# A decoder block on one core: tokens placed 32 bytes below the weights' phase, V's weight rows padded to 320, the root's table loaded ahead, and two steps of the first MLP chunk moved

## The chip, the cores and the metric

The kernel runs on one core of one Trainium2 chip. Its time is the device time of one execution in microseconds; a run's figure is the median of several executions. Nearly all matrix products take float32r operands, each split into a high and a low part, and add three products of these parts.

## The reference

One layer of a hybrid decoder on 512 tokens of width 1024, all in float32. What is computed, cut to what matters here:

```python
h = rms_norm(x, norm_mix)
proj = h @ w_in                       # split into u, q, six k/v pieces, g_nsa, g_merge
y_pool = pool_mixer(u, w_pool, pool_scale)
y_nsa = nsa_mixer(q, kc, vc, ks, vs, kw, vw, g_nsa, ...)   # compressed, selected, window branch
g_a, g_b = split(sigmoid(g_merge))
merged = g_a * (y_pool @ w_proj_pool) + g_b * (y_nsa @ w_proj_nsa)
x = x + merged @ w_out
h = rms_norm(x, norm_mlp)
x = x + square(relu(h @ w_ff1)) @ w_ff2          # 1024 -> 4096 -> 1024
return rms_norm(x, norm_final)
```

## The kernel before

The work runs in three stages on one TensorE instruction stream. **Stage 1** (to about 167 us) normalizes x, turns it into columns (R1 holds the high parts, R2 the low parts of all 8 row blocks of 512 tokens) and multiplies it by the columns of `w_in`. **Stage 2** (to about 378 us) is the attention, with the products for the merge gates filled in between. **Stage 3** forms the merged activations, multiplies them by `w_out` (the layer "o"), normalizes (lines 1416 to 1437) and runs the MLP in four chunks `c` of 1024 hidden columns.

Each product is written as TensorE's three terms (high by high, high by low, low by high; `split_products`, line 403). The output projection and both MLP products use a Strassen-Winograd scheme: an operand's four quarters 11, 12, 21, 22 and their sums T1 to T4 meet the weights' quarters A11, A12, A21, A22 and the sums S1 to S4, in seven products instead of eight. In an MLP chunk the first product (`Group`, line 1507; `product`, line 1494) runs for two groups `g` of 512 hidden columns each: the weights are the stationary operand, the tokens the moving one in pieces of 256 columns, 24 matmuls per product, all issued by line 1526. The second one (`Wide`, line 1265; line 1290) has the hidden activations stationary and the weights moving, 512 columns at a time.

**Weights.** `WL` (line 91) lists the weights in the order of use, `LD` the loads. `emit_load` (line 220) starts a DMA on SP's queue into a tile of 1024 elements per partition, of a ring of `RAW` = 4 tiles and a fifth in stage 3 (line 1240); a tile comes free by `give_back`. `emit_prep_half` (line 328) splits a landed weight: ACT copies the high part (line 358, or 312 for the MLP's), DVE or POOL subtracts for the low part (360, 314). `ahead` (line 375) does this up to three weights before their use. Some S sums are made ahead in DRAM by DMAs with addition (line 275); others are made in place, by adding a held raw tile to the next (line 324): A12 and S2 of a group are added to give S4. In the first chunk the order of use is A11, A12, S1, S3, S2 for both groups, then A22 and S4 of one group after the other (line 134).

**Where the operands lie.** The constants' pool holds, in this order, `ident`, two small tiles, R1, R2, `MA` and `GB` (16,384 bytes per partition each), `identR`; then come the raw ring and the weights' high and low tiles. R1 and R2 each have `STEP` = 32 elements more than their 8 x 512. Stage 1 reads R1 from its start and R2 from 128 bytes on; stage 3 (`Rf`, line 1237) reads R1 from 128 bytes on and R2 from its start. T2, T3 and T4 have tiles of their own (line 1486), the first with the same 32 elements ahead of it. V's weights are three tiles with rows of 304 elements (line 111; the products are `project_v`, line 830).

**The end of the output projection.** `by_tile` (line 1300) does the last products of the projection tile by tile; after each, `to_fm` (line 1416) takes the square sums, the root (`normed`, line 1249: `Sqrt` on ACT, `reciprocal` on DVE, two multiplications on DVE by line 1255), eight transposes on TensorE (1426) and the splits of their results. `sums_x` (line 1439) then forms T1, T3, T2 and T4 of the tokens: a difference or sum on DVE (1443), the high part on ACT (1444), the low part on DVE (1446).

**The group's rest.** `Group.main` (line 1538) waits for S1, S2 and S3, then forms u2 (line 1546) and u3 (1547) on DVE; A22 adds onto the bank that u3 reads, so it waits for u3 (`NEEDS`, line 1534) and for T4.

**What sets the order.** The generators in `side` are stepped between matmuls (`step_side`, line 417), which gives the order in which instructions are written. The framework's planner then puts each engine's instructions in order by this priority and by its own costs and due times; `tc.issue_after(x)` pins what is written inside it behind `x` on `x`'s engine. A function needing another table on ACT gets a load of that table in front of it.

Of the kernel before, what the change touches and what calls it, by code (L numbers as in the profile page):

```python
# [13 lines left out]
F32 = mybir.dt.float32  # L14
# [13 lines left out]
LAG, PLAG = 5, 2  # L28
P_BUFS, PT_BUFS = 6, 3
CMP_AT = 4  # L30
STEP = 32
BIG = 1e30
EPS = 1e-6

# [29 lines left out]
def trunk(ctx: ExitStack, tc: tile.TileContext, A, out):  # L64
# [17 lines left out]
    ident = cp.tile([128, 128], F32, name="ident")  # L82
    eps_t = cp.tile([128, 1], F32, name="eps_t")
    tick = cp.tile([128, 1], F32, name="tick")
    RR = [cp.tile([128, 8 * S + STEP], FR, name=n) for n in ("R1", "R2")]
    R1, R2 = (R[:, i * STEP:i * STEP + 8 * S].rearrange("p (j t) -> p j t", j=8) for i, R in enumerate(RR))
    MA = cp.tile([128, 8, S], F32, name="MA")
    GB = cp.tile([128, 8, S], F32, name="GB")
    GBf = GB.rearrange("p j t -> p (j t)")
# [104 lines left out]
    for c in range(4):  # L194
# [16 lines left out]
            turn.append((g, o))  # L211
        add_turn(2, c, of, turn)
    dest = {}

    raws, hls = {}, {}
    st = {"load": 0, "prep": 0, "use": 0, "kept": 0, "pairs": 0, "sums": 0, "hold": 0}
    spare, slots_hl = [], []
    held, begun = {}, deque()

    def emit_load():  # L220

        i = st["load"]
        if i >= len(LD):
            return False
        segs = LD[i]
        a = segs[0][0].shape[1]
        b = sum(s.shape[2] for s, _ in segs)
        assert a * b <= 1024
        if not by_name() or st["kept"] < RAW:
            st["kept"] += by_name()  # L230
            t = wp.tile([128, 1024], F32, tag="raw", bufs=RAW, name=f"raw{i}")
        elif spare:
            t = spare.pop(0)
        else:
            return False
        st["load"] += 1
        v = t[:, :a * b].rearrange("p (a b) -> p a b", a=a)
        for s, o in segs:
            began = nc.sync.dma_start(v[:, :, o:o + s.shape[2]], s)
        raws[i] = (t, a, b)  # L240
        for _ in range(sums_after(i)):
            make_sum(began)
        if i >= len(P1) + len(FILL2) + 4 and (len(begun) > 2 or begun and st["sums"] == len(jobs)):
            add_sum()
        return True
# [49 lines left out]
    def group_steps(i):  # L295

        key, at = WL[i]
        if i in PLUS:
            while st["load"] <= PLUS[i]:
                assert emit_load()  # L300
            t = raws.pop(PLUS[i])[0]
            DVE.tensor_tensor(t, t, held[key], op=ALU.add)
            give_back(held.pop(key))
            yield
        elif isinstance(at, str):
            t = held.pop(key)
        else:
            while st["load"] <= at:
                assert emit_load()
            t = raws.pop(at)[0]  # L310
        h, l = slot_of(i)
        ACT.activation(h, t, AF.Copy)  # L312
        yield
        DVE.tensor_tensor(l, t, h.bitcast(F32), op=ALU.subtract)  # L314
        a = 2 if key[-3] == "2" else 4
        hls[i] = tuple(x.rearrange("p (a b) -> p a b", a=a) for x in (h, l))
        to = SUM_OF.get(key)
        if to is None:
            give_back(t)
        elif to not in held:  # L320
            held[to] = t
        else:
            yield
            DVE.tensor_tensor(t, t, held[to], op=ALU.add)
            give_back(held[to])
            held[to] = t

    def emit_prep_half():

        i = st["prep"]  # L330
        if i >= len(WL):
            return
        if WL[i][0][0] in "AS":
            if "gen" not in part:
                part["gen"] = group_steps(i)
            if next(part["gen"], True):
                part.clear()
                st["prep"] += 1
            return
        at = WL[i][1]  # L340
        if "h" not in part:
            while st["load"] <= at:
                assert emit_load()
            if WL[i][0] in dest:
                h, l = dest[WL[i][0]][:2]
            else:
                h, l = slot_of(i)
            part.update(h=h, l=l, half=0)
        h, l = part["h"], part["l"]
        t, a, b = raws[at]  # L350
        n = a * b
        cut = (a // 2) * b
        sl = slice(0, cut) if part["half"] == 0 else slice(cut, n)
        if sl.stop > sl.start:
            if mode["first"] is POOL:
                POOL.tensor_scalar(h[:, sl], t[:, sl], 1.0, 1.0, op0=ALU.mult, op1=ALU.mult)
            else:
                ACT.activation(h[:, sl], t[:, sl], AF.Copy)  # L358
            eng = POOL if mode["first"] or part["half"] and mode["pool"] else DVE
            eng.tensor_tensor(l[:, sl], t[:, sl], h[:, sl].bitcast(F32), op=ALU.subtract)  # L360
        if part["half"] == 0:
            part["half"] = 1
            return
        part.clear()
        st["prep"] += 1
        raws.pop(at)
        if st["load"] > RAW + MLP0:
            give_back(t)
        else:
            emit_load()  # L370
            if st["kept"] == RAW:
                give_back()
        hls[i] = (h[:, :n].rearrange("p (a b) -> p a b", a=a), l[:, :n].rearrange("p (a b) -> p a b", a=a))

    def ahead():

# [857 lines left out]
    XQ = {b: quarter(MAf, i) for i, b in enumerate(("11", "12", "21", "22"))}  # L1234
    XT = quarter(GBf, 0)
    have = set()
    Rf = [R[:, STEP - i * STEP:STEP - i * STEP + 8 * S] for i, R in enumerate(RR)]
    XB = {b: [quarter(f, i) for f in Rf] for i, b in enumerate(("11", "21", "22", "T1"))}
    slots_hl.insert(0, [p4.tile([128, 1024], FR, name=f"w3{e}") for e in "hl"])
    give_back(p4.tile([128, 1024], F32, name="raw5"))  # L1240
# [111 lines left out]
    with ExitStack() as c3:  # L1352
# [13 lines left out]
            return x.rearrange("p (h t) -> p h t", h=2)  # L1366

        def split(x, hi, lo):
            ACT.activation(hi, x, AF.Copy, scale=0.5)
            DVE.scalar_tensor_tensor(lo, x, 0.5, hi.bitcast(F32), op0=ALU.mult, op1=ALU.subtract)  # L1370

        def split_m(j):
            x, n = GB[:, j, :], j % 4
# [4 lines left out]
            y = GB[:, n, 256:]  # L1378
            DVE.tensor_tensor(y, x[:, 256:], y, op=ALU.subtract)
            split(two(x), *(m[:, :, n, :] for m in M2))  # L1380
            split(y, *(m[:, n, :] for m in MB["T3"]))

        def split_t(j):
            x, n = GB[:, j, :], j % 4
# [14 lines left out]
        for j in range(2, 8):  # L1399
            def post(ps, j=j):  # L1400
                merge(j, ps)
                for n in (0, 1) if j == 2 else (j - 1,):
                    split_m(n)
                if j > 2:
                    split_t(j - 3)
                if j == 7:
                    split_m(7)
            fm3(f"pn{j}", post, OT)
        formed.update(("11", "21", "22", "T1", "T3"))
        side.append(rest())  # L1410
# [28 lines left out]
        def sums_x():  # L1439

            for o, d, x, y in (("T1", XT, XQ["11"], XQ["12"]), ("T3", XQ["12"], XQ["22"], XQ["12"]),
                               ("T2", XQ["11"], XQ["22"], XT), ("T4", XQ["21"], XQ["11"], XQ["21"])):
                DVE.tensor_tensor(d, x, y, op=ALU.add if o == "T2" else ALU.subtract)
                ACT.activation(XB[o][0], d, AF.Copy)
                yield
# [40 lines left out]
    for b in ("T2", "T3", "T4"):  # L1486
        XB[b] = []
        for e in "HL":
            n = STEP if b + e == "T2H" else 0
            t = a4.tile([128, 1024 + n], FR, name=f"x{b}{e}")  # L1490
            XB[b].append(t[:, n:].rearrange("p (k t) -> p k t", k=4))
    YF = {"11": quarter(GBf, 0), "12": quarter(GBf, 1), "21": quarter(GBf, 2), "22": quarter(MAf, 1)}
# [14 lines left out]
    class Group:  # L1507
# [30 lines left out]
        def main(self):  # L1538
# [4 lines left out]
            while not {"S1", "S2", "S3"} <= self.done:  # L1543
                yield
            yield
            DVE.tensor_tensor(self.u2, self.s, self.ps["b"], op=ALU.subtract)
            DVE.tensor_tensor(self.u3, self.ps["c"], self.u2, op=ALU.add)
            self.done.add("u3")
            yield
            DVE.tensor_tensor(self.u3, self.ps["d"], self.u3, op=ALU.add)  # L1550
# [186 lines left out]
```

## Time and profile before

| | |
|---|---|
| median of 3 runs | 787.26 us (786.75 to 787.62) |
| the profiled execution | 787.36 us |
| its span, from the first to the last instruction | 785.5 us |
| TensorE matmul, busy | 765.9 us (98%), 4517 matmuls |
| VectorE, busy | 639.4 us (81%) |
| ScalarE, busy | 498.9 us (64%) |
| GpSimd, busy | 186.4 us (24%) |
| mean granted TensorE clock | 0.996 |

A row of the timeline gives the start in us from the span's start, the duration in us, the engine, the line, the operation, the output and the inputs with the shapes, and in brackets the idle time before it with what ended it. Rows of one kind that follow each other are merged (x2 and so on). Matmuls are pipelined and their ends are modelled, so their durations overlap; the pace is the distance of two starts. A row of the table by windows gives the window, its length, each engine's busy time and instructions, the granted clock of TensorE, the DMA engines' share and GB/s.

### The profile page before, as it was taken

Reading aid. Unit: us, or ns where it says so; the run is one execution under the profiler, and the core shown is the slowest. Engines: PE = TensorE matmul, PEld = TensorE weight load, DVE = VectorE, ACT = ScalarE, POOL = GpSimd, SP = SyncE. Lnnn points to the kernel's source line nnn. Section 1 sums busy time; section 2 is a strip of 40 time slices with the busy share of each in tenths; the row PEclk is TensorE's granted clock in tenths of the full one; section 3 lists DMA queues with packets and bytes.
Section 4 is the critical chain, followed back from the end, with each engine's and each line's share of the span. In section 5 each row is a group of like instructions: output and inputs, shape, how many; then the busy total and the mean of one; then the engine's idle time right before and its main releaser. Section 6 shows DMA issues by size and latency. Waiting matters only on the chain. (4 is left out here: it accounts for less than half of the span.)

```text
span 785.5 us, 12873 instructions
## 1 busy us (share of the span) xinstructions
PE 765.9 (98%) x4517; PEld 671.2 (85%) x4517; DVE 639.4 (81%) x1207; ACT 498.9 (64%) x970; POOL 186.4 (24%) x253
## 2 busy tenths in 40 slices
PE   8999999999999999999999899999999999999995
PEld 6889888888888888988887799979998999799974
DVE  6788666436999888897698999997899789978897
ACT  6756543335998888897346685944783478346755
POOL 4000000026766776673110100111111101000002
PEclk9999999999999999999999999999999999999999
DMA  9454743487655866434997978989897989785552
GB/s 306 136 158 121 185 125 104 125 216 213 135 118 126 166 151 135 114 82 78 360 264 221 285 188 234 300 227 295 257 290 226 292 255 280 182 268 163 165 184 108
DMA packets 120156, 153.88 MB, mean 196 GB/s; under 512 B 5878, under 2 KB 88474, under 8 KB 119835
## 3 DMA queue, kind: packets, MB, share of 16 engines
q1 hardware_dynamic: 99514, 125.06, 48.6%
q0 software_dynamic: 20288, 27.27, 22.5%
q8 instruction: 36, 0.59, 0.3%
q10 hardware_dynamic: 288, 0.72, 0.3%
q14 instruction: 30, 0.24, 0.1%
HBM read 148.31 MB, written 56.62 MB: 261 GB/s over the span
## 5 line engine op out<-in xcount | busy, mean ns | idle before, releaser
L401 PE MATMUL psF<-R,wh 128*128 128x512 f32 x512 | 162.2, 398 | 0.0
L312 ACT ACTIVATE wh<-raw 128x1024 fp32r<-128x1024 f32 x84 | 88.5, 1056 | 80.6 <-PE psB L1526 28.2
L314 DVE TENSOR_TENSOR wl<-raw,wh 128x1024 fp32r<-128x1024 f32 x84 | 103.7, 1239 | 23.8 <-ACT wh L312 23.8
L279 POOL DMA_DIRECT2D S<-w_ff x44 | 48.6, 1104 | 292.0 <-DMA S<-w_ff 191.6
L401 PEld LDWEIGHTS psF<-R,wh 128*128 128x128 f32 x512 | 92.1, 188 | 16.3
L401 PE MATMUL psF<-R,wl 128*128 128x512 f32 x256 | 100.2, 392 | 0.0
L1085 POOL TENSOR_SCALAR P<-P,sm,GT 128x128 f32<-128x128 f32 (+3 forms) x128 | 82.6, 666 | 53.6 <-DVE sm L1075 37.6
L358 ACT ACTIVATE wh<-raw 128x512 fp32r<-128x512 f32 (+1 forms) x90 | 54.5, 620 | 62.1 <-PE psF L401 44.0
L1069 ACT ACTIVATE P<-P,sm 128x128 f32<-128x128 f32 (+3 forms) x128 | 71.1, 558 | 10.1 <-DVE sm L1059 9.4
L312 ACT ACTIVATE w3h<-raw 128x1024 fp32r<-128x1024 f32 x42 | 44.4, 1058 | 43.8 <-PE psB L1526 14.3
L360 DVE TENSOR_TENSOR wl<-raw,wh 128x512 fp32r<-128x512 f32 (+1 forms) x75 | 52.2, 700 | 20.7 <-ACT wh L358 20.6
L1059 DVE CUSTOM_DVE_ANT_0 P<-psS,cst 128x128 f32<-128x128 f32 (+3 forms) x128 | 59.7, 483 | 8.1 <-PE psT L1102 6.1
L1526 PE MATMUL psB<-R,wh 128*128 128x256 f32 x352 | 64.5, 283 | 0.0
L1117 DVE TENSOR_TENSOR PT<-psT,PT 128x512 fp32r<-128x512 f32 (+2 forms) x96 | 56.6, 596 | 3.8 <-ACT PT L1113 3.0
L314 DVE TENSOR_TENSOR w3l<-raw,w3h 128x1024 fp32r<-128x1024 f32 x42 | 51.2, 1218 | 8.4 <-ACT w3h L312 8.4
L401 PEld LDWEIGHTS psF<-R,wl 128*128 128x128 f32 x256 | 48.0, 188 | 10.4
L1113 ACT ACTIVATE PT<-psT 128x512 fp32r<-128x512 f32 (+2 forms) x96 | 49.4, 519 | 8.8 <-PE psT L1102 7.8
L1526 PEld LDWEIGHTS psB<-R,wh 128*128 128x128 f32 x352 | 54.7, 189 | 0.2
L1102 PE MATMUL psT<-ident,P 128*128 128x128 f32 x320 | 50.9, 273 | 1.1 <-DVE PT L1117 1.1
L1526 PE MATMUL psB<-R,wl 128*128 128x256 f32 x176 | 50.0, 284 | 0.0
L1102 PEld LDWEIGHTS psT<-ident,P 128*128 128x128 f32 x320 | 39.5, 140 | 10.0 <-issue 1.8
L1136 PE MATMUL psO<-PT,VV 128*128 128x256 f32 x320 | 47.7, 286 | 0.0
(451 smaller groups left out, 2010.0 us busy)
## 6 DMA issues: line engine op xcount, KB each, us to landing
raw<-w_ff SPq DMA_DIRECT2D x54, 512.0 KB, 6.0
S<-w_ff POOLq DMA_DIRECT2D x44, 512.0 KB, 8.3
raw<-S SPq DMA_DIRECT2D x44, 512.0 KB, 5.7
raw<-w_in SPq DMA_DIRECT2D x32, 512.0 KB, 4.1
S<-w_ff SPq DMA_DIRECT2D x32, 512.0 KB, 7.4
S<-S SPq DMA_DIRECT2D x12, 512.0 KB, 5.8
S_2o<-w_out POOLq DMA_DIRECT2D x8, 512.0 KB, 6.6
raw<-w_proj_nsa SPq DMA_DIRECT2D x8, 512.0 KB, 5.2
```

The costliest lines, as they stand in the source:

```text
L312: ACT.activation(h, t, AF.Copy)
L314: DVE.tensor_tensor(l, t, h.bitcast(F32), op=ALU.subtract)
L358: ACT.activation(h[:, sl], t[:, sl], AF.Copy)
L360: eng.tensor_tensor(l[:, sl], t[:, sl], h[:, sl].bitcast(F32), op=ALU.subtract)
L401: PE.matmul(ps, a, b, start=first and j == 0, stop=last and j == n - 1, skip_group_check=True)
L1059: DVE.tensor_tensor_reduce(out=P[:, o:o + n].rearrange("p (a c) -> p a c", c=128), in0=s, in1=m, scale=1.0, scalar=3e38, op0=ALU.add, op1= ...
L1069: last_exp[:] = [ACT.activation(c, c, AF.Exp, bias=sm[:, 0, e:e + 1], scale=-1.0, accum_out=sm[:, 1, e:e + 1])]
L1085: r = POOL.tensor_scalar(P[:, o:o + n], P[:, o:o + n], sm[:, 2, e:e + 1], GT[:, qb, c + e:c + e + 1], op0=ALU.mult, op1=ALU.mult)
L1102: PE.transpose(pt[:, 128 * j:128 * j + 128], P[:, 128 * j:128 * j + 128], ident)
L1113: ACT.activation(dH, src, AF.Copy)
L1117: DVE.tensor_tensor(dL, src, dH.bitcast(F32), op=ALU.subtract)
L1526: PE.matmul(out, w[u][:, k, 128 * f:128 * f + 128], XB[x][v][:, k, :], **kw)
```

## The change

It has five parts.

- **Addresses.** `STEP` is 8 elements (32 bytes). R1 gets 64 elements more than 8 x 512, R2 gets 8. Stage 1 reads both from 32 bytes on, stage 3 reads both from their starts. T2's own tile has 56 elements ahead of it, so that all seven token operands keep one phase.
- **V's rows.** A weight's rows are laid out at a stride rounded up to 64 elements: V's 304 become 320. The halves of a split are now whole rows. For all other weights the stride is what it was.
- **The root's table.** Behind the ACT part of the last `split_m` of the projection (the split of T3, for j = 7) a `Sqrt` of one column is written, which brings the table load with it.
- **A12's first weight** (A12 of chunk 0, group 0) is loaded into `GBf[:, 1024:2048]`, rows 2 and 3 of the gates' buffer, and no longer into a tile of the ring; its load is pinned behind the load before it. After S2 has been added to it, that place is not given to the ring.
- **T4 later.** T4's three steps are written only after S2 of the first group has been taken into use. And u2 of chunk 0's second group is pinned behind u3 of its first.

```diff
-STEP = 32
+STEP = 8
...
-    RR = [cp.tile([128, 8 * S + STEP], FR, name=n) for n in ("R1", "R2")]
-    R1, R2 = (R[:, i * STEP:i * STEP + 8 * S].rearrange("p (j t) -> p j t", j=8) for i, R in enumerate(RR))
+    RR = [cp.tile([128, 8 * S + n], FR, name=f"R{i + 1}") for i, n in enumerate((64, STEP))]
+    R1, R2 = (R[:, STEP:STEP + 8 * S].rearrange("p (j t) -> p j t", j=8) for R in RR)
...
+    names = [k for k, _ in WL]
+    AFTER_T2 = names.index("S2100") + 1
+    APART = dict(WL)["A12100"]
...
+    def stride(b):
+        return (b + 63) // 64 * 64
...
-        if not by_name() or st["kept"] < RAW:
+        if i == APART:
+            t = GBf[:, 1024:2048]
+        elif not by_name() or st["kept"] < RAW:
...
-        v = t[:, :a * b].rearrange("p (a b) -> p a b", a=a)
+        v = t[:, :a * stride(b)].rearrange("p (a b) -> p a b", a=a)
         for s, o in segs:
-            began = nc.sync.dma_start(v[:, :, o:o + s.shape[2]], s)
+            with tc.issue_after(last_load[0].ins) if i == APART else nullcontext():
+                began = nc.sync.dma_start(v[:, :, o:o + s.shape[2]], s)
+        last_load[:] = [began]
...
             DVE.tensor_tensor(t, t, held[to], op=ALU.add)
-            give_back(held[to])
+            if to != "S4100":
+                give_back(held[to])
...
-        n = a * b
-        cut = (a // 2) * b
-        sl = slice(0, cut) if part["half"] == 0 else slice(cut, n)
+        h, l, t = (x[:, :a * stride(b)].rearrange("p (a b) -> p a b", a=a)[:, :, 0:b] for x in (h, l, t))
+        sl = slice(0, a // 2) if part["half"] == 0 else slice(a // 2, a)
...
-    Rf = [R[:, STEP - i * STEP:STEP - i * STEP + 8 * S] for i, R in enumerate(RR)]
+    Rf = [R[:, 0:8 * S] for R in RR]
...
                 if j == 7:
-                    split_m(7)
+                    with behind(split_m(7)):
+                        ACT.activation(tick, eps_t, AF.Sqrt)
...
                                ("T2", XQ["11"], XQ["22"], XT), ("T4", XQ["21"], XQ["11"], XQ["21"])):
+                if o == "T4":
+                    yield
+                    while st["use"] < AFTER_T2:
+                        yield
                 DVE.tensor_tensor(d, x, y, op=ALU.add if o == "T2" else ALU.subtract)
...
-            n = STEP if b + e == "T2H" else 0
+            n = 64 - STEP if b + e == "T2H" else 0
...
-            DVE.tensor_tensor(self.u2, self.s, self.ps["b"], op=ALU.subtract)
-            DVE.tensor_tensor(self.u3, self.ps["c"], self.u2, op=ALU.add)
+            with tc.issue_after(gs[0].made.ins) if self.c == 0 and self.g else nullcontext():
+                DVE.tensor_tensor(self.u2, self.s, self.ps["b"], op=ALU.subtract)
+            self.made = DVE.tensor_tensor(self.u3, self.ps["c"], self.u2, op=ALU.add)
```

More of the change, by code (lines that the diff above doesn't have):

```diff
@@ L217, in trunk @@
     spare, slots_hl = [], []
-    held, begun = {}, deque()
+    held, begun, last_load = {}, deque(), []
+    def stride(b):
+        return (b + 63) // 64 * 64
     def emit_load():
@@ L227, in emit_load @@
         b = sum(s.shape[2] for s, _ in segs)
-        assert a * b <= 1024
-        if not by_name() or st["kept"] < RAW:
+        assert a * stride(b) <= 1024
+        if i == APART:
+            t = GBf[:, 1024:2048]
+        elif not by_name() or st["kept"] < RAW:
             st["kept"] += by_name()
@@ L350, in emit_prep_half @@
         t, a, b = raws[at]
-        n = a * b
-        cut = (a // 2) * b
-        sl = slice(0, cut) if part["half"] == 0 else slice(cut, n)
[L354 to L360, printed above, removed]
+        h, l, t = (x[:, :a * stride(b)].rearrange("p (a b) -> p a b", a=a)[:, :, 0:b] for x in (h, l, t))
+        sl = slice(0, a // 2) if part["half"] == 0 else slice(a // 2, a)
+        if mode["first"] is POOL:
+            POOL.tensor_scalar(h[:, sl], t[:, sl], 1.0, 1.0, op0=ALU.mult, op1=ALU.mult)
+        else:
+            ACT.activation(h[:, sl], t[:, sl], AF.Copy)
+        eng = POOL if mode["first"] or part["half"] and mode["pool"] else DVE
+        eng.tensor_tensor(l[:, sl], t[:, sl], h[:, sl].bitcast(F32), op=ALU.subtract)
         if part["half"] == 0:
@@ L365, in emit_prep_half @@
         st["prep"] += 1
-        raws.pop(at)
+        t = raws.pop(at)[0]
         if st["load"] > RAW + MLP0:
@@ L372, in emit_prep_half @@
                 give_back()
-        hls[i] = (h[:, :n].rearrange("p (a b) -> p a b", a=a), l[:, :n].rearrange("p (a b) -> p a b", a=a))
+        hls[i] = (h, l)
     def ahead():
@@ L1368, in split @@
         def split(x, hi, lo):
-            ACT.activation(hi, x, AF.Copy, scale=0.5)
+            r = ACT.activation(hi, x, AF.Copy, scale=0.5)
             DVE.scalar_tensor_tensor(lo, x, 0.5, hi.bitcast(F32), op0=ALU.mult, op1=ALU.subtract)
+            return r
         def split_m(j):
@@ L1380, in split_m @@
             split(two(x), *(m[:, :, n, :] for m in M2))
-            split(y, *(m[:, n, :] for m in MB["T3"]))
+            return split(y, *(m[:, n, :] for m in MB["T3"]))
         def split_t(j):
```

## The prediction

> **What bounds the kernel now.** I read the page first, then the list of TensorE's waits over the stage around the first MLP chunk (370 to 540 us), then the table by windows, and last the timelines of PE, ACT and DVE at each wait.
>
> ```profile
> span 785.5 us, 12873 instructions
> PE 765.9 (98%) x4517; PEld 671.2 (85%) x4517; DVE 639.4 (81%) x1207; ACT 498.9 (64%) x970; POOL 186.4 (24%) x253
> ```
>
> The profiled execution took 787.36 us, so 1.86 us lie around its span; the median of the three runs, 787.26, is 0.1 below it. TensorE is the bound, but it is busy by the record even where it crawls, so I look for matmuls that start later than their pace allows. The waits in the stage that the change touches are four, one place each:
>
> ```profile
> PE psB L1426 <- DVE xs L1255: 2.2, 1, 2.2
> PE psB L1526 <- DVE MA L1547: 0.7, 1, 0.7
> PE psB L1526 <- ACT w3h L312: 0.6, 1, 0.6
> PE psB L1290 <- DVE yT3L L1581: 0.5, 1, 0.5
> ```
>
> The columns are the sum, the number and the longest, in us. The first is the transposes of the normed activations; it is followed by a stretch at a lower clock. In the table by windows the column before the last two is the granted clock:
>
> ```profile
> 441.50:444.10 2.60, 0.36 (x3) 0.05 (x1) 2.60 (x6) 2.10 (x7) 0.00 (x0) 1.00 1.11 253
> 444.10:448.50 4.40, 4.40 (x19) 3.66 (x20) 3.54 (x7) 2.51 (x5) 0.00 (x0) 0.61 1.06 343
> ```
>
> During the wait DVE is busy for all 2.60 us: DVE, not a transfer, is what TensorE waits for. Right behind it the clock is 0.61.
>
> **The change part by part. Addresses.** The sizes of the tiles, in order of allocation, give the distances. Before, R1 and R2 are 16,512 bytes each; everything from there to the weights adds multiples of 256, so the tokens of an MLP chunk's first product start 128 bytes (modulo 256) from the weights. After, R1 is 16,640 and R2 16,416 bytes, all that follows moves by 32, and these tokens start 32 bytes below the weights' phase, which is the title's 224. Everywhere else the distance stays, but for the identity of the transposes and for V, whose rows of 304 elements (1,216 bytes) ran through several phases and now keep one. What is a phase worth? The pace is read from starts:
>
> ```profile
> 617.68 0.40 PE L1526 MATMUL psB<-R,wh 128*128 128x256 f32 x2
> 658.00 0.39 PE L1290 MATMUL psB<-wh,y11H 128*128 128x512 f32 x1
> 96.80 1.11 PE L727 MATMUL psC<-wkt,cA 128*128 128x256 f32 x8
> 97.76 0.63 PE L401 MATMUL psF<-R,wh 128*128 128x512 f32 x2
> 212.54 0.88 PE L1136 MATMUL psO<-PT,VV 128*128 128x256 f32 x6
> 213.26 0.39 PE L1034 MATMUL psS<-KH,Q 128*128 128x512 f32 x1
> 64.50 0.45 PE L401 MATMUL psV<-wh,R 128*128 128x304 f32 x2
> 64.92 0.44 PE L401 MATMUL psV<-wh,R 128*128 128x304 f32 x2
> ```
>
> From 617.68 to 658.00 lie the 336 matmuls of one first product (2 groups, 7 products of 24), at distance 128: 40.32 / 336 = 120.0 ns. The eight of line 727 stand at distance 0: 0.96 / 8 = 120.0 ns. The six of line 1136 stand at 96: 0.72 / 6 = 120.0 ns. Three matmuls of V, at mixed phases, take 0.42 us, 140.0 ns each, and 304 against 256 columns is just the 20.0 ns that 48 columns cost at 0.417 ns. So three phases show the same pace to the digit, and V none of its own. Distance 224 isn't in the trace. I take 0 for it; the bounds I keep are 5 ns each way (a quarter of the step between the 120 and the 140 rows, an estimate), which over 4 x 336 = 1344 matmuls is 6.7 us. V's splits and loads keep their counts and elements: 0.
>
> [...]
>
> **The root's table.** On ACT the square root's table is loaded in front of line 1251; the change loads it some 29 us earlier, behind the last product's T3 split.
>
> ```profile
> 411.76 1.05 ACT L312 ACTIVATE w3h<-raw 128x1024 fp32r<-128x1024 f32 x1
> 414.97 1.22 DVE L314 TENSOR_TENSOR w3l<-raw,w3h 128x1024 fp32r<-128x1024 f32 x1
> 440.39 1.28 ACT L1251 ACT_TABLE_LOAD   x1
> 441.68 0.29 ACT L1251 ACTIVATE sq<-sq 128x1 f32<-128x1 f32 x1
> 440.86 0.68 DVE L1325 TENSOR_TENSOR x<-x,psB 128x512 f32<-128x512 f32 x1
> 441.46 1.22 DVE L314 TENSOR_TENSOR wl<-raw,wh 128x1024 fp32r<-128x1024 f32 x1
> 442.60 0.15 DVE L1252 RECIPROCAL sq<-sq 128x1 f32<-128x1 f32 x1
> 443.25 1.41 DVE L1255 SCALAR_TENSOR_TENSOR xs<-x,sq,gB 128x512 f32<-128x512 f32 x2
> 441.43 0.39 PE L1290 MATMUL psB<-w3h,mT1L 128*128 128x512 f32 x1
> 444.05 0.76 PE L1426 MATMUL psB<-ident,xs 128*128 128x128 f32 x4 [2.24 <-DVE xs L1255]
> 449.10 0.60 PE L1426 MATMUL psB<-ident,xs 128*128 128x128 f32 x4
> 449.46 0.47 PE L1290 MATMUL psB<-w3h,mT1H 128*128 128x512 f32 x1
> 450.24 0.39 PE L1312 MATMUL psB<-wh,m2H 128*128 128x512 f32 x1
> ```
>
> TensorE's next start comes 2.62 us after 441.43, where a 512-column matmul paces at 120.0 + 256 x 0.417 = 226.7 ns: 2.39 us lost. From 444.05 to 450.24 it then runs 12 wide matmuls and 16 transposes in 6.19 us; at full clock these are 12 x 0.227 + 4 x 0.36 (449.10 to 449.46) = 4.16 us: 2.03 more lost, to the low clock. Together 4.4 us hang on one normalization.
>
> Taking 1.28 us off ACT's chain doesn't by itself move DVE, whose reciprocal stands behind a weight split that ends just as it starts. But the order on each engine is a planner's, by its costs: with the root due at 440.4 instead of 441.7 I expect the reciprocal ahead of that split, behind the 0.68 us of line 1325 at the latest. Then it runs at 441.5, the first half of xs ends at about 442.3, and the transposes start at 442.3 instead of 444.05: the wait shrinks by 1.8 us, and the clock doesn't drop. Saved at that place: 1.8 + 2.0 = 3.8 us. The split that is pushed back is for the product that starts at 450.24. What the edit adds is a 0.29 us activation and the 1.28 us load at about 412, on ACT; queued behind them is the split at 411.76, for which DVE's low half comes 2.2 us after it ends: cover for the 1.6 us, so 0; were it gone, up to 1.6 us.
>
> [...]
>
> **T4 later, A12's first weight elsewhere.** Two waits follow in the first chunk.
>
> ```profile
> 475.13 1.05 ACT L1444 ACTIVATE xT4H<-MA 128x1024 fp32r<-128x1024 f32 x1
> 477.76 1.06 ACT L312 ACTIVATE w3h<-raw 128x1024 fp32r<-128x1024 f32 x1
> 476.44 1.21 DVE L1446 TENSOR_TENSOR xT4L<-MA,xT4H 128x1024 fp32r<-128x1024 f32 x1
> 478.04 0.28 PE L1526 MATMUL psB<-xT2L,wh 128*128 128x256 f32 x1
> 478.87 0.39 PE L1526 MATMUL psB<-xT2H,w3h 128*128 128x256 f32 x1 [0.56 <-ACT w3h L312]
> 483.42 1.06 ACT L312 ACTIVATE wh<-raw 128x1024 fp32r<-128x1024 f32 x1 [4.61 <-DMA raw<-w_ff]
> 486.26 1.22 DVE L314 TENSOR_TENSOR wl<-raw,wh 128x1024 fp32r<-128x1024 f32 x1
> 487.39 0.68 DVE L1547 TENSOR_TENSOR MA<-psB,MA 128x512 f32<-128x512 f32 x1
> 487.26 0.28 PE L1526 MATMUL psB<-xT2H,w3l 128*128 128x256 f32 x1
> 488.22 0.36 PE L1526 MATMUL psB<-xT4H,wh 128*128 128x256 f32 x1 [0.68 <-DVE MA L1547]
> 441.50:488.10 46.60, 43.20 (x56) 0.96 0.80 209
> ```
>
> S2's second weight waits for ACT: 0.83 - 0.12 = 0.7 us. T4's three steps (1.05 on ACT; its low half and its difference, about 1.21 each, on DVE) stand ahead of it; moved behind S2's first use they free ACT 1.05 us sooner, so that wait goes: -0.7. Their new place is ACT's 4.61 us wait for a DMA, which covers the 1.05; the 2.4 us on DVE come due before A22 at 488, their user.
>
> A22 waits 0.96 - 0.12 = 0.84 us, for u3, which stands behind weight splits whose raw weights landed late. A12100 in the gates' buffer, whose last readers are the splits of T's rows at the start of the output projection, leaves the ring of raw tiles one place, so every later load of that ring on SP's queue is issued one place earlier, until S2's sum has read it; splits then fall into the gap before 483.42, and u3 runs sooner: -0.8. No transfer is added. The pinned order of the second group's u2 behind the first group's u3 is the order that already runs: 0.
>
> **The sum.** At their places 3.8 + 0.7 + 0.8 = 5.3 us. But DVE is behind all of them: in the last row above it works 43.20 of the 46.60 us up to A22 and takes no step less, so A22 can't come more than 3.4 us earlier, save for steps that can wait. I take 3.2: 787.36 - 3.2 = 784.16 for this execution, 784.1 by the median. From A22 on the lead is kept, since DVE's own queue is then as far ahead.
>
> **The rivals.** A change of 0.2%, 1.6 us, is about what the measurement can tell from none.
>
> 1. The reciprocal keeps its place behind the split, or DVE takes the lead back before A22: only part of the two small waits goes, 0 to 1.5 us, so about 786.7. For it speaks that DVE has no gap at all in the 2.60 us of the wait; against it that the load is the one long step between sum and root. Chance 0.18.
> 2. Slower: T4 comes late. Its chain, 1.21 + 1.05 + 1.21 = 3.5 us, now starts when S2 starts, at 477.9 at the earliest, and shares DVE with weight splits, the sums into raw tiles, u2 and u3. Up to 488.07, where u3 ends, there are 10 us for it. From the point where its low half ends after u3, each us of it is a us for TensorE; if it falls behind u3 and one split, A22 starts 2.4 us later than before, and as DVE sets that start, the time saved earlier is waited off there; half of a low clock (1.0) may follow. 787.3 + 2.4 = 789.7 or so. Chance 0.16.
> 3. Distance 224 changes the pace of the first products. 5 ns less: 784.1 - 6.7 = 777.4; 5 ns more: 790.8. For it speaks only that the distance is untried here; against it the equal rows at three phases. Chance 0.14 for less, 0.03 for more.
> 4. [...] Chance 0.09.
>
> **How the numbers follow.** The forecast, 784.1 with its own range of 782.9 to 785.5, has 0.40. Faster by over 0.2% (below 785.7) take the forecast, rival 3's gain and most of rival 4: 0.62. Within: rival 1 and the rest of 4: 0.19. Slower: rivals 2 and 3's loss: 0.19. The range of eight in ten runs from 778.2, short of the full gain of rival 3, to 788.6, into rival 2.
>
> **What would show it.** Right: three table loads still, but none after 415; transposes that follow the last wide matmul by under a microsecond, and no row with a clock below 1 between 435 and 460; the S2 weight and A22 without a wait of 0.5 us; a first product of 336 matmuls that still takes 40.3 us. Wrong: a first product of another length by more than 0.5 us (rival 3); the reciprocal still behind a split (rival 1); a wait of A22 for xT4L (rival 2). If all of these come right and the end doesn't move by 2 us, the step that failed is the lead kept past A22.

## The result and the profile after

The changed kernel takes 782.61 us (median of 6 runs, 782.1 to 783.3) against 787.4 us of the kernel before, measured alongside: a ratio of 0.994, with a 95% interval of 0.9927 to 0.9953, so 4.8 us less. The profiled execution took 783.30 us with a span of 781.5 us, against 787.36 and 785.5. One execution in the study, the first profiled one of the addresses alone, ran at a mean granted clock of 0.85 and took 836.76 us; no figure here uses it. Lines below the first edits have moved: 1426 is now 1437, 1526 is 1541, 1547 is 1563, 1255 is 1264, 1252 is 1261, 1251 is 1260, 1290 is 1299.

TensorE's waits over the stage of the first MLP chunk, in the same view as before:

```profile
PE psB L1541 <- DVE MA L1563: 1.4, 1, 1.4
PE psB L1437 <- DVE xs L1264: 0.5, 1, 0.5
PE psB L1299 <- DVE yT3L L1597: 0.5, 1, 0.5
PE psB L1541 <- DVE R L1461: 0.2, 1, 0.2
```

The wait in front of the transposes fell from 2.2 to 0.5 us and S2's wait is gone, but A22's wait for u3 doubled, from 0.7 to 1.4. The timelines of ACT, DVE and TensorE show the normalization:

```profile
417.65 1.28 ACT L1418 ACT_TABLE_LOAD   x1
440.90 0.28 ACT L1260 ACTIVATE sq<-sq 128x1 f32<-128x1 f32 x1
441.49 0.16 DVE L1261 RECIPROCAL sq<-sq 128x1 f32<-128x1 f32 x1
442.14 1.41 DVE L1264 SCALAR_TENSOR_TENSOR xs<-x,sq,gB 128x512 f32<-128x512 f32 x2
443.54 1.21 DVE L324 TENSOR_TENSOR wl<-raw,wh 128x1024 fp32r<-128x1024 f32 x1
442.05 0.39 PE L1299 MATMUL psB<-w3h,mT1L 128*128 128x512 f32 x1
442.95 0.66 PE L1437 MATMUL psB<-ident,xs 128*128 128x128 f32 x4 [0.51 <-DVE xs L1264]
443.36 0.48 PE L1299 MATMUL psB<-wh,mT1H 128*128 128x512 f32 x1
443.68 0.39 PE L1299 MATMUL psB<-wl,mT1H 128*128 128x512 f32 x1
447.57 0.40 PE L1321 MATMUL psB<-wh,m2H 128*128 128x512 f32 x1
```

The root runs with no load in front of it, the reciprocal runs ahead of the weight split (now at 443.54), and the transposes start 0.90 us after the last wide matmul in place of 2.62. The table by windows (the granted clock is the column before the last two) has the stretch behind the wait, and DVE's work up to u3:

```profile
444.00:448.50 4.50, 4.50 (x28) 3.64 (x27) 4.50 (x7) 4.45 (x9) 0.00 (x0) 1.00 1.11 267
441.50:485.50 44.00, 41.91 (x313) 38.98 (x311) 43.53 (x57) 33.83 (x53) 4.64 (x4) 1.00 0.91 251
```

No low clock, and DVE works 43.53 of 44.00 us, where it had been 43.20 of 46.60: its gaps are used up. Last, one first product of 336 matmuls (chunk 2), by its first row and the row that follows it:

```profile
615.27 0.40 PE L1541 MATMUL psB<-R,wh 128*128 128x256 f32 x2
655.03 0.40 PE L1299 MATMUL psB<-wh,y11H 128*128 128x512 f32 x1
```

39.76 us in place of 40.32, 118.3 ns a matmul in place of 120.0.

Two effects are thus seen: a lead of some 3.2 us won around the first chunk, and 0.56 us in each first product of chunks 1 to 3. All the kernels below are compared by the same marks, taken from the starts of the same matmuls in every trace: a, from the last wide matmul ahead of the transposes (441.43 before) to the first matmul of chunk 0's first product; b, from there to A22; c, a and b together; d, the 96 matmuls of 256 columns from A22 to the chunk's second product; e, the first products of chunks 1 to 3 together. In us:

| kernel | a | b | c | d | e |
|---|---|---|---|---|---|
| before | 14.28 | 32.52 | 46.79 | 11.46 | 120.95 |
| addr_again (addresses) | 12.72 | 33.34 | 46.06 | 11.44 | 119.28 |
| t4a12_alone | 14.29 | 31.97 | 46.26 | 11.48 | 120.95 |
| table_alone | 10.97 | 33.58 | 44.54 | 11.47 | 120.95 |
| table_t4 | 10.97 | 33.06 | 44.02 | 11.47 | 120.95 |
| table_a12 | 10.95 | 32.91 | 43.86 | 11.47 | 120.95 |
| sched (table, T4, A12) | 10.97 | 32.60 | 43.57 | 11.47 | 120.95 |
| after | 10.99 | 32.62 | 43.61 | 11.44 | 119.28 |
| d64 (after, distance 64) | 10.97 | 32.62 | 43.59 | 11.38 | 118.73 |
| d192 (after, distance 192) | 10.97 | 32.61 | 43.59 | 12.86 | 118.72 |

### The profile page after: what moved, and what is told of

Same layout as the page of the kernel before. It is cut to its first block, busy times and chain, and to the rows that moved or that the text cites. A ratio compares the mean times of both kernels' runs of the same rounds, so it can differ in the third digit from the quotient of the medians.

```text
span 781.5 us, 12874 instructions
## 1 busy us (share of the span) xinstructions
PE 763.0 (98%) x4517; PEld 668.3 (86%) x4517; DVE 639.5 (82%) x1207; ACT 498.4 (64%) x971; POOL 186.5 (24%) x253
## 5 line engine op out<-in xcount | busy, mean ns | idle before, releaser
L322 ACT ACTIVATE w3h<-raw 128x1024 fp32r<-128x1024 f32 x42 | 44.5, 1059 | 46.3 <-PE psB L1299 17.9
```

## The experiments

The theory behind them: the table wins the wait and the low clock at the transposes, T4 and A12 let DVE keep that lead to A22, and the distance of 224 bytes is what makes the first products shorter. The rivals: the shorter products come from V's rows or from the moved steps; the table alone wins everything; the distance does nothing and the steps all of it.

**table_alone.** The kernel before with the root's table loaded ahead, nothing else.

```diff
-                    split_m(7)
+                    with behind(split_m(7)):
+                        ACT.activation(tick, eps_t, AF.Sqrt)
```

> Before, with the root's table loaded ahead and nothing else. Theory: the transposes start under 1 us after the wide matmul before them, no row of a clock below 1 there, and 3.3 us are gained by the start of the first MLP chunk; DVE then sets A22's start, so that 2 to 3 us are kept at the end. Rival, that only a part of 1.3 us is the table's and the low clock has another cause: the clock falls below 1 again near 445 us and 1.3 us are gained.

Measured: 785.12 us, ratio 0.9972 (0.9961 to 0.9983). Mark a falls by the full 3.3 us, but b grows by 1.06: of what is won at the transposes, a third is gone again before A22, where TensorE waits 0.7 us for u3, 0.4 and 0.3 us for high copies of weights on ACT and 0.2 us for R, against 0.7 for u3 and 0.6 for one high copy in the kernel before.

**t4a12_alone.** T4 written later, A12's first weight in the gates' buffer, and the pin of u2; the table as before.

```diff
+        if i == APART:
+            t = GBf[:, 1024:2048]
...
-            give_back(held[to])
+            if to != "S4100":
+                give_back(held[to])
...
+                if o == "T4":
+                    yield
+                    while st["use"] < AFTER_T2:
+                        yield
```

> Before, with T4 later, A12's first weight in the gates' buffer and the pinned u2; no table, no addresses. Theory: the 0.7 us wait of S2's second weight goes, A22's wait doesn't grow by more than that since TensorE arrives no earlier from the wait at 441 us, and 0.3 to 1.5 us are gained. Rival: T4's low half and u3 come later than before on a DVE without gaps, A22's wait grows by over 0.7 us, and the time is the same or up to 1 us more.

Measured: 785.9 us, ratio 0.9981 (0.9969 to 0.9993). Its waits in the stage, the start of A22, and u3:

```profile
PE psB L1435 <- DVE xs L1264: 2.2, 1, 2.2
PE psB L1539 <- ACT w3h L320: 1.1, 1, 1.1
488.36 0.36 PE L1539 MATMUL psB<-xT4H,wh 128*128 128x256 f32 x1 [1.09 <-ACT w3h L320]
487.53 0.69 DVE L1561 TENSOR_TENSOR MA<-psB,MA 128x512 f32<-128x512 f32 x1
```

S2's wait is gone. The 1.1 us are A22's, where it had waited 0.7: the profile puts them down to a weight's high copy on ACT, but u3 ends only 0.1 us ahead of A22's start too. So b falls by 0.55 only, and this kernel keeps the wait at the transposes (2.2 us) and, by its mark a of 14.29 where the kernel before has 14.28, the low clock behind it.

**sched.** All of the steps (table, T4, A12, the pin) with the addresses and V's rows of before.

> Before, with the table ahead, T4 later, A12's first weight apart and the pinned u2, and with the addresses and V's rows as before. Theory, that the parts add up because T4 and A12 pay DVE's part of the table's gain: 3.3 us gained up to the first MLP chunk, and from there to the chunk's second product 44.0 us or less where the table alone needs 45.05; each later first product 40.32 us; 3.0 to 4.0 us less than before. Rival, that the table alone holds all of the schedule's gain: as the table alone, 2.2 us less, with 45 us on that stretch.

Measured: 783.49 us against 787.2, ratio 0.9955 (0.9942 to 0.9967). Its marks a to d are those of the full change within 0.04 us, and e is that of the kernel before: the steps make the lead, and none of the pace.

**table_t4 and table_a12.** The table with T4's steps and the pin, or with A12's place, one execution each.

> The table ahead with T4 later and the pinned u2, A12's weight in the ring. Theory, that T4's two DVE steps are what keeps the lead: the stretch from the start of the first chunk to its second product takes 44.1 us as with both, 45.05 with the table alone. Rival, that the ring's extra place does it: 45 us.

> The table ahead with A12's first weight in the gates' buffer; T4 where it was, no pin. Theory as before: the stretch from the start of the first chunk to its second product takes about 45 us, since DVE has the same work in the same places. Rival, that the ring's extra place keeps the lead: 44.1 us.

Single times of 785.74 and 784.76 us. Mark b is 33.06 and 32.91, between 33.58 (table only) and 32.60 (both): they bring back 0.52 and 0.67 of the 0.98 us that DVE takes of the table's lead. From the chunk's start to its second product the two need 44.5 and 44.4 us (b and d together), so neither the theory nor the rival of these two expectations holds: T4 and A12 each do a part. In table_t4 A22 waits 1.8 us for u3:

```profile
PE psB L1534 <- DVE MA L1556: 1.8, 1, 1.8
```

**addr_alone and addr_again.** The kernel before with the new places of the tokens only, first for its time, then once more for its profile.

```diff
-    RR = [cp.tile([128, 8 * S + STEP], FR, name=n) for n in ("R1", "R2")]
+    RR = [cp.tile([128, 8 * S + n], FR, name=f"R{i + 1}") for i, n in enumerate((64, STEP))]
...
-    Rf = [R[:, STEP - i * STEP:STEP - i * STEP + 8 * S] for i, R in enumerate(RR)]
+    Rf = [R[:, 0:8 * S] for R in RR]
```

> Before, with the addresses alone: STEP 8, the two offsets of R1 and R2, T2's own offset; V's rows, the table, A12 and T4 as before. Theory: the 336 matmuls of a first product take 39.75 us instead of 40.31 in each of chunks 1 to 3, and the wait at 441 us with its low clock stays at 2.2 us; time 2 us less (1.7 from three chunks and up to 0.5 from chunk 0). Rival, as predicted: 40.3 us per product and 0 within 0.5 us.

> The kernel before with the new places of the tokens and nothing else (V's rows, the table, A12, T4 and the pin as before), for its profile. If the distance sets the pace, the first products of chunks 1 to 3 take 39.76 us each, as in the changed kernel, and the second products, the transposes' wait of 2.2 us and the stretch at a low clock behind it stay as before; span about 784.3 to 784.8 us, against 785.5. If the pace in the changed kernel came from V's rows or from the moved steps, the first products stay at 40.32 us.

Measured: 786.22 us, ratio 0.9985 (0.9972 to 0.9997), and a span of 782.8 us in the profile. The first product of chunk 2 there:

```profile
617.14 0.40 PE L1526 MATMUL psB<-R,wh 128*128 128x256 f32 x2
656.90 0.40 PE L1290 MATMUL psB<-wh,y11H 128*128 128x512 f32 x1
```

39.76 us: the pace comes from the addresses and from nothing else in the change. But the expectation had the low clock stay, and it didn't. The transposes wait as long as in the kernel before, and the stretch behind runs at full clock:

```profile
444.48 0.66 PE L1426 MATMUL psB<-ident,xs 128*128 128x128 f32 x4 [2.24 <-DVE xs L1255]
```

```profile
444.52:448.92 4.40, 4.40 (x28) 3.73 (x29) 4.28 (x8) 3.68 (x7) 0.00 (x0) 1.00 1.10 266
```

So a wait of 2.2 us is followed by a low clock in two traces (0.61 in the kernel before; t4a12_alone, by its mark a) and by none in a third. This gives the price of the drop: mark a is 14.28 with it and 12.72 without, 1.56 us; of these only 0.73 reach A22 (c: 46.79 and 46.06), because TensorE then waits longer for S2's weight, 1.0 us instead of 0.6, and for u3, 1.5 us instead of 0.7:

```profile
PE psB L1526 <- DVE MA L1547: 1.5, 1, 1.5
PE psB L1526 <- ACT w3h L312: 1.0, 1, 1.0
```

**pace.** A kernel that leaves out the whole computation and only measures the disputed cost: groups of 33 matmuls, a new weight at each, at sixteen distances, with 256 columns and with 512.

```diff
+        for n in (256, 512):
+            for d in range(0, 64, 4):
...
+                for j in range(COUNT):
+                    w = j % 8
+                    nc.tensor.matmul(t[:, 0:n], W[:, 128 * w:128 * w + 128], X[:, d:d + n], start=j == 0,
+                                     stop=j == COUNT - 1, skip_group_check=True)
```

> Leaves out the whole computation: after a warm-up of 40 matmuls it runs, for 256 and then for 512 columns, 16 groups of 33 matmuls, each with freshly loaded weights, whose moving operand starts 0, 16, 32 ... 240 bytes (modulo 256) from the weights; nothing else runs. Theory, that the distance by itself sets the pace: at 256 columns 120.0 ns at distances 0, 96 and 128 and 118.3 ns at 224, so that a group of 32 gaps at 224 is 0.05 us shorter than one at 128. Rival, that the 1.7 ns came from the buffers that moved by 32 bytes against the other engines or the DMAs: all 16 distances alike, within 0.2 ns. At 512 columns either 226.7 ns at all distances, or 1.7 ns less at 224 if the distance acts per weight load.

The first row of a group and of the one after it, for distances 0 (pa), 64 (pe), 128 (pi), 192 (pm) and 224 (po):

```profile
17.14 0.64 PE L35 MATMUL pax<-X,W 128*128 128x256 f32 x4
21.10 0.41 PE L35 MATMUL pbx<-X,W 128*128 128x256 f32 x2
...
32.78 0.39 PE L35 MATMUL pex<-X,W 128*128 128x256 f32 x2
36.52 0.39 PE L35 MATMUL pfx<-X,W 128*128 128x256 f32 x2
...
48.21 0.40 PE L35 MATMUL pix<-X,W 128*128 128x256 f32 x2
52.12 0.40 PE L35 MATMUL pjx<-X,W 128*128 128x256 f32 x2
...
63.83 0.40 PE L35 MATMUL pmx<-X,W 128*128 128x256 f32 x2
67.60 0.40 PE L35 MATMUL pnx<-X,W 128*128 128x256 f32 x2
...
71.53 0.40 PE L35 MATMUL pox<-X,W 128*128 128x256 f32 x2
75.44 0.40 PE L35 MATMUL ppx<-X,W 128*128 128x256 f32 x2
```

Divided by 33: 120.0, 113.3, 118.5, 114.2 and 118.5 ns. The distance does change the pace, by up to 6.7 ns in 120, with nothing else running. But 128 and 224 are the same here, where the kernel has 120.0 and 118.3. With 512 columns the order is another one: within the groups 226.7 ns at distance 0 and 229 to 235 at the others.

**d64 and d192.** By that measurement two other distances promise more, so the changed kernel was run with the tokens 64 and 192 bytes from the weights. The diff is that of d64; d192 has 16 and 48 exchanged.

```diff
-    RR = [cp.tile([128, 8 * S + n], FR, name=f"R{i + 1}") for i, n in enumerate((64, STEP))]
-    R1, R2 = (R[:, STEP:STEP + 8 * S].rearrange("p (j t) -> p j t", j=8) for R in RR)
+    RR = [cp.tile([128, 8 * S + n], FR, name=f"R{i + 1}") for i, n in enumerate((16, 48))]
+    R1, R2 = (R[:, n:n + 8 * S].rearrange("p (j t) -> p j t", j=8) for R, n in zip(RR, (0, 48)))
...
-    Rf = [R[:, 0:8 * S] for R in RR]
+    Rf = [R[:, n:n + 8 * S] for R, n in zip(RR, (16, 0))]
...
-            n = 64 - STEP if b + e == "T2H" else 0
+            n = 16 if b + e == "T2H" else 0
```

> The changed kernel with one thing else: the tokens of the first MLP products lie 64 bytes (modulo 256) above the weights, where the changed one has 224; stage 1 stays at distance 0. Theory, that the distance by itself sets the pace, as in the run that measures it alone (113.3 ns at 64, 118.5 at 224): 336 matmuls take 38.1 us instead of 39.76, and the three chunks that TensorE bounds give 5 us more, 777.6 against 782.6. Rival, that with the other engines at work the distance is worth only the 1.7 ns seen, or that DVE and the DMAs, now nearer to the bound, take the gain back as waits: 39.8 us per product, or 38.1 us with the second products longer by as much, and 782 us.

> The changed kernel with the tokens of the MLP's first products 192 bytes from the weights in place of 224. By the earlier measurement alone (114.2 ns at 192 against 118.5 at 224) the 336 matmuls of one of these products would take 38.4 us. By the scale at which the kernel itself answered to distance 64 (117.8 ns where the measurement had 113.3) they take 39.5 to 39.7 us, against 39.76 at 224 and 40.32 at 128. If the distance were not what moved the pace of these products, but something else in the new layout, they stay at 39.76.

d64 takes 781.76 us against 787.2, ratio 0.9938 (0.9925 to 0.9952): the lowest time of the study, not to be told from the change's 0.9927 to 0.9953. In both kernels a first product of chunks 1 to 3 takes 39.58 us, 117.8 ns a matmul, and not the 38.1 to 38.4 us of the earlier measurement. d192, a single execution, took 784.28 us, and shows a second thing. A22 waits 2.1 us for u3, and behind that wait the clock is halved:

```profile
485.43 0.55 PE L1540 MATMUL psB<-xT4H,wh 128*128 128x256 f32 x1 [2.14 <-DVE MA L1562]
```

```profile
485.30:488.70 3.40, 3.27 (x15) 3.30 (x16) 3.00 (x4) 1.26 (x2) 0.00 (x0) 0.50 1.09 210
```

Mark d, where the other kernels have 11.4, is 12.86. Mark c is the same 43.59: DVE sets when A22 starts, so a TensorE that runs ahead of it only waits longer, 2.1 us here and 1.5 in d64, and behind the 2.1 the clock was 0.50.

**pace2 and pace3.** Two more kernels without the computation ask why 192 bytes gave 114.2 ns there and 117.8 in the kernel. pace2 has the first product's own order (each high weight twice in a row, the moving operand from two tiles), and repeats some distances while DVE and ACT work without a break.

```diff
+        KERNEL = [(k, u, v) for k in range(4) for u, v in ((0, 0), (0, 1), (1, 0))]
+        OTHER = [(k, u, u) for k in range(6) for u in range(2)]
...
+        for i in range(28):
+            nc.vector.tensor_tensor(o, raw, raw, op=mybir.AluOpType.subtract)
+            nc.scalar.activation(o2, raw, mybir.ActivationFunctionType.Copy)
```

> A kernel that leaves out the whole computation: groups of 49 matmuls of 256 columns in the order of the first product (high by high, high by low, low by high: each high weight is loaded twice in a row, the moving operand comes from two tiles), at sixteen distances (tiles ka to kp); five distances (0, 64, 128, 192, 224) with a new weight at each matmul and the two moving tiles in turn (oa, oe, oi, om, oo); and the five in the kernel's order while VectorE and ScalarE work without a break on tiles of their own (ba, be, bi, bm, bo). Theory A, the order of the operands sets what a distance is worth: the groups k give the kernel's own figures, 120.0 ns at 128, 118.3 at 224, 117.8 at 64, and the groups o give those of the earlier measurement, 118.3, 118.5 and 113.3. Theory B, the other engines' accesses do: the groups k give 118.3 at 128 and 113.3 at 64, and the groups b are slower, near 120 and 118. Theory C, neither: k, o and b are all as in the earlier measurement, and the rest lies in the kernel's own offsets from one k to the next.

Groups of 49 in the kernel's order at distances 64 (ke) and 192 (km), each with the row that follows it, and 192 again beside the busy engines (bm):

```profile
42.03 0.28 PE L37 MATMUL ke<-XH,WH 128*128 128x256 f32 x1
47.80 0.28 PE L37 MATMUL kf<-XH,WH 128*128 128x256 f32 x1
...
88.36 0.28 PE L37 MATMUL km<-XH,WH 128*128 128x256 f32 x1
93.94 0.28 PE L37 MATMUL kn<-XH,WH 128*128 128x256 f32 x1
...
157.59 0.28 PE L37 MATMUL bm<-XH,WH 128*128 128x256 f32 x1
163.14 0.28 PE L37 MATMUL bo<-XH,WH 128*128 128x256 f32 x1
```

117.8, 113.9 and 113.3 ns. At 128 and 224 the groups have 118.5 and 118.5 in the kernel's order, 118.6 and 118.2 in the other, 118.6 and 118.2 beside DVE and ACT. So neither the order nor the other engines matter to more than 0.6 ns: theories A and B fall, and C holds but for one distance: 64 now has 117.8 to 117.9 ns in every group, where pace had 113.3.

pace3 moves the operand by multiples of 256 bytes and changes the step from weight to weight:

```diff
+        for way, ws in (("s", range(8)), ("l", range(0, 8, 2)), ("r", (0, 0, 4, 1, 1, 5, 2, 2, 6, 3, 3, 7))):
...
+                for i, at in enumerate((0, 64, 128, 192, 256, 512)):
```

> A kernel that leaves out the whole computation: groups of 25 matmuls of 256 columns, a new weight at each, at distances 64, 128 and 192 (tiles with a, b, c as second letter); within each, the moving operand starts 0, 256, 512, 768, 1024 or 2048 bytes further on (third letter u to z), which leaves the distance modulo 256 as it is. First letter s: the weights follow each other 512 bytes apart; l: 1024 bytes apart; r: an order in which a weight is loaded twice, then one 2048 bytes away. Theory A, only the distance modulo 256 counts: the six groups of a distance agree within 0.5 ns, at 113.3, 118.3 and 114.2 ns, and so do s, l and r. Theory B, more bits of the two addresses count: the groups of a distance fall into two or three levels, 113 to 114 and near 118 for distance 64 and 192, 118.3 and near 120 for 128, which would give the kernel's 117.8 and 120.0 a place.

All eighteen groups at distance 64 lie at 117.8 to 117.9 ns, the eighteen at 128 at 118.4 to 118.8, the six at 192 at 113.3. Moves by 256 to 2048 bytes and the other steps of the weights change the pace by 0.4 ns at most, so theory B falls here, and theory A holds but for its figures at 64 (113.3) and 192 (114.2). The first group at 64 has its weights and its moving operand in the same places as the group of pace that ran at 113.3.

The kernels' own traces show that one distance has two paces there too. These rows are the first ones of two products that follow each other in chunk 0, 24 matmuls apart, in the kernel before (distance 128) and in d192:

```profile
474.84 0.28 PE L1526 MATMUL psB<-xT3H,w3h 128*128 128x256 f32 x1
477.68 0.28 PE L1526 MATMUL psB<-xT3H,wh 128*128 128x256 f32 x1
...
477.69 0.28 PE L1540 MATMUL psB<-xT2H,wh 128*128 128x256 f32 x1
480.41 0.28 PE L1540 MATMUL psB<-xT2H,w3h 128*128 128x256 f32 x1
```

They are 118.3 and 113.3 ns a matmul, the figures of the measurement alone, where the same kernels have 120.0 and 117.8 in chunks 1 to 3. In d192 the 113.3 ns last from 467.6 to 483.0 us, from one wait of TensorE to the next, beside the other engines' work, and behind the wait for u3 the pace is 117.8 again. That lead is why its A22 waits 2.1 us where that of d64 waits 1.5. So 64, 128 and 192 bytes each had two paces; in these traces the pace changes only where the stream of matmuls is interrupted, and then holds, for 336 matmuls in chunks 1 to 3. What picks the pace at an interruption stays open. Order, other engines, larger offsets and the weights' step, changed one at a time in the kernels that measure alone, moved it by 0.6 ns at most.

## Why the prediction was right, and where not

**The time.** The 782.61 us measured lie 0.3 below the forecast's own range of 782.9 to 785.5; what it had wrong is the part of the addresses.

**The bound: right.** The prediction capped 5.3 us of local gains at the 3.4 us of gaps that DVE had, and took 3.2. Mark c fell by 3.18. DVE's idle time up to u3 went from 3.40 to 0.47 us, and every kernel with table, T4 and A12 has c between 43.57 and 43.61, whatever TensorE's pace.

**The table: right, one term too large.** The reciprocal came ahead of the split, so rival 1 fell; it came even sooner than foreseen, 0.56 us before the start of the last wide matmul (441.49 against 442.05) and not 0.07 behind it (441.5 against 441.43), but 0.67 us of line 1334 stand between it and xs on DVE (441.56). The wait shrank by 1.73 us (1.8 foreseen). The low clock was put at 2.03 us and is worth 1.56. What was mis-sized is the full-clock time of that stretch: 12 wide matmuls and 16 transposes were put at 4.16 us and take 4.62 (442.95 to 447.57 after). Most of it is the first wide matmul behind each four transposes, which takes 0.32 us (443.36 to 443.68) and not the 0.227 put down for all. The load sits at 417.65, not by 415, and costs TensorE nothing: from the first wide matmul of the projection to the last one ahead of the transposes it needs 30.43 us, and 30.44 before.

**T4 and A12: right in sum, wrong place by place.** Foreseen were 0.7 us at S2 and 0.8 at A22. Without the table they bring 0.53 (c of t4a12_alone), with it 0.97. S2's wait went; A22's didn't go but grew from 0.7 to 1.4 us. This is not rival 2: T4's low half ends before u3 begins, and A22 waits for u3.

```profile
481.84 1.22 DVE L1461 TENSOR_TENSOR xT4L<-MA,xT4H 128x1024 fp32r<-128x1024 f32 x1
484.82 0.69 DVE L1563 TENSOR_TENSOR MA<-psB,MA 128x512 f32<-128x512 f32 x1
```

It is the cap seen from TensorE: the two local prices should have been dropped once the cap bound them. That the wait for A22 would vanish was a sign wrongly named for a step that otherwise held.

**The addresses: wrong.** The step that failed is "three phases show the same pace to the digit, so I take 0 for it". The row of 336 matmuls was right, and equal rows at 0, 96 and 128 would say nothing of 224 in any case. But the two others couldn't have shown a difference of this size: they are eight and six matmuls long, and 0.01 us, the last digit of a row, is 1.3 and 1.7 ns a matmul there. Distance 224 has 118.3 ns, 1.7 less than 120.0 and inside the 5 ns of bound: rival 3's gain, at a third of its size. Of 4 x 0.56 us only three count: in chunk 0 the kernel before has about 118.5 already, so d is 11.46 before and 11.44 with the addresses, and mark b is 32.62 in the change and 32.60 in sched. Since 128 had 118.5 ns too (in chunk 0), the runs show that the new places bring the shorter products, but not whether by their distance itself or by which pace is picked.

A price of 0 for the addresses doesn't hold: e is 120.95 in the kernel before and 119.28 with the addresses, and the groups of pace differ by up to 6.7 ns with nothing else running. By what means the distance acts, no run here shows.

**V's rows: no run of their own.** They were put at 0. The 96 matmuls of V take 14.48 us in the two kernels after and d64, and 14.65 before, in sched and in addr_again: 0.17 us.

**The lead past A22: right.** From A22 to the last matmul sched needs 288.36 us, the kernel before 288.61; the change needs 287.18, lower by the pace. The forecast of 784.1 is thus 1.5 us above the 782.61 measured, about the three products' 1.7.

**The clock, rival 4.** That the clock drops all the same, for 785.3 us, was the author's estimate, and no run shows such a drop: in the change the wait at that place is 0.51 us and the clock 1.00 from 435 to 460 us, and mark a is 10.95 to 10.99 in all seven kernels with the table ahead. But in the kernel before, the drop isn't a fixed cost: addr_again has the wait without it. The traces show where the two differ. In the kernel before the granted clock falls at 444.47, rises at 447.88 and falls again at 782.39: half clock for 3.413 us, then full clock for 334.51, which is 98.0 times as long. By the clock's record in the traces the full clock ahead of the drop lasts 433.49 us, 127.0 times 3.413, and that of the change 764.59 us, 224.0 times. Counted back and forth in steps of 3.413 us from a change of the clock, each trace can be cut into periods, an estimate where no change is near. The first two pairs of rows are the period of the wait and the next one, in the kernel before and in addr_again. Then comes the period of d192's wait, whose half clock is shown above, and at last a period near the end of the kernel before, with full clock behind it.

```profile
441.06:444.47 3.41, 1.17 (x9) 0.69 (x7) 3.41 (x6) 2.54 (x7) 0.00 (x0) 1.00 1.12 272
444.47:447.88 3.41, 3.41 (x13) 2.76 (x12) 2.77 (x6) 1.98 (x4) 0.00 (x0) 0.50 1.08 356
...
440.52:443.93 3.41, 1.72 (x8) 1.00 (x6) 3.41 (x7) 2.90 (x7) 1.03 (x1) 1.00 1.08 342
443.93:447.34 3.41, 2.86 (x19) 2.48 (x20) 3.41 (x7) 2.69 (x7) 0.00 (x0) 1.00 1.12 250
...
481.88:485.29 3.41, 1.41 (x13) 1.21 (x11) 3.38 (x5) 1.06 (x1) 0.41 (x1) 1.00 0.79 261
...
775.57:778.98 3.41, 1.54 (x13) 1.34 (x12) 3.31 (x8) 3.21 (x11) 0.00 (x0) 1.00 0.38 154
```

TensorE is idle for 2.24 us of the first period and for 2.00 of d192's, and half clock follows for one period. In addr_again the same wait of 2.24 us lies across a border, 1.69 us on one side, and the clock stays; so it does after the 1.87 us of the last row. If the wait falls anywhere in a period alike, the kernel before has the drop in about half of its executions, an estimate: the wait lies inside one period or passes a border by up to 0.24 us, (1.17 + 2 x 0.24) / 3.41 = 0.48. That share can't be read from their times. So the 3.2 us are in part luck: the profiled execution had the drop, and against the 46.06 of addr_again, without it, the change's mark c is only 2.45 lower.

**The parts and the whole.** One by one: addresses 1.2, table 2.2, T4 and A12 1.5 us, in sum 4.9 for a measured 4.8. That they add up is chance in part: table, T4 and A12 together bring c 3.22 us, more than 2.25 and 0.53, and of the four first products that the addresses touch three gain.

## What to carry to other kernels

Before local gains are added up, sum the busy time of the engine behind them over the whole stretch: its gaps were the most that could be won here (3.18 of 3.40 us), and a wait changed place rather than vanish (S2's 0.6 us went, A22's grew from 0.7 to 1.4). A price that isn't in the trace isn't shown to be 0 by neighbours that are equal; a kernel of a few groups measures it alone, and still has to be tried in place, since the 113 to 114 ns measured alone became 117.8 in most of the product. A row of a few matmuls, printed to 0.01 us, can't show a difference of 1 or 2 ns a matmul. A wait of 2 us on TensorE is worth removing for more than its length, as the clock may be halved behind it (0.50 behind 2.24 us in the kernel before and behind 2.14 in d192, 1.00 behind 2.24 in addr_again), but how much of that counts was set by the next engine in line: of 1.56 us, 0.73 reached A22.

## What the runs showed of the hardware

- The pace of float32r matmuls with a new weight at each went with the distance of the moving operand from the weights modulo 256 bytes. Alone, at 256 columns, it ran from 113.3 to 120.0 ns (pace); in the products of chunks 1 to 3 it was 120.0 at 128 (before), 118.3 at 224 (after), 117.8 at 64 (d64) and at 192 (d192). Moving the operand by 256 to 2048 bytes changed nothing (within 0.4 ns, pace3).
- One distance had two paces. At 64 bytes it was 113.3 ns in pace and 117.8 in pace2 and pace3, in the latter with both operands in the same places; at 192 it was 113.3 and 117.8 in one trace (d192), at 128 about 118.5 and 120.0 (the kernel before). In these traces the change came where the stream of matmuls was interrupted; what picks the pace wasn't found.
- At 512 columns distance 0 was the fastest of sixteen, 226.7 ns, and the others took 229 to 235 (pace). At 256 columns the same distance was the slowest, 120.0: what suited one width didn't suit the other.
- The stretches of one granted clock were multiples of 3.413 us: 127, 1 and 98 of them in the kernel before, 224 in the change. Half clock for one such period came behind periods in which TensorE was idle for 2.24 us (the kernel before) and 2.00 us (d192), and not behind 1.87 (the kernel before) or 1.69 us (addr_again). So a wait of 2.24 us that lay across a border cost no clock in addr_again.
